# Two layers with 32 experts each: returned rows in the weight stream, one block per expert, selection matmuls for the last four pairs

## The chip, the core and the metric

The kernel runs on one core of a Trainium2 chip. The metric is device time in microseconds. A core has a matmul engine (PE; PEld is its weight load), a vector engine (DVE), a scalar engine (ACT), GpSimd (POOL) and a queue engine (SP) that issues most of the DMAs; a suffix q, as in DVEq, means that engine's own sequencer. Matmuls write to PSUM banks (tiles named `ps` and `psg`).

## The reference, cut to what matters

Two layers work on 512 latent tokens and 256 context tokens of width 1024. Each layer has a mixer (Fourier and convolution in the first, attention in the second) and then a mixture of experts. Layer 0 sends all 768 tokens through the experts, layer 1 only the 512 latent ones. Each token picks a group of 8 experts out of 4 and the best 2 inside it:

```python
h2 = rmsnorm(x, norm_ffn_g[layer]) * (1.0 + sc2) + sh2
...
g_idx = jnp.argmax(g_logit, axis=-1).astype(jnp.int32)
...
top_v, top_i = lax.top_k(e_logit, TOP_K)          # TOP_K = 2, inside the group
w = (g_prob * jax.nn.softmax(top_v, axis=-1)).astype(h.dtype)
...
def expert_block(args):
    xblk, e = args
    return (jax.nn.silu(xblk @ w_gate[e]) * (xblk @ w_up[e])) @ w_down[e]
...
return jnp.zeros((n_tok + 1, d), h.dtype).at[row_tok].add(yb * row_w[:, None])[:n_tok]
...
x = x + g2 * out[: b * s].reshape(x.shape)
```

An expert has 1024 x 512 gate, 1024 x 512 up and 512 x 1024 down weights in f32: two slots of 2 MB (2.10 million bytes) for gate and up, one for down. The 32 experts of a layer are 201 MB. After the second layer comes a final norm.

## The kernel before

The function `moe` (from L869) does the expert part of one layer. It keeps the tokens transposed in `XT` (rows called `xt` in the trace) and puts the normed tokens row by row into a table `h2d` in HBM, whose row 0 is zeros. The router gives every expert 64 slots in a pair's block of 128 rows; `idi` holds, for each pair and slot, the row of `h2d`, 0 for an empty slot. What does not fit into 64 slots goes into the other half of a pair's block a second time (`overflow`) or, beyond that, into spill blocks.

**Weights.** `load_parts` (L960) issues the weights in pinned program order on SP into a ring of eight slots of 2 MB (tiles named `ring`). Per pair of experts the order is gate/up (two slots) of the first, gate/up of the second, down of the first, down of the second. A load waits until the slot it takes is free, and holds all later DMAs of SP's queue. The last three slots of a layer come in halves of 1 MB.

**A pair** (the loop at L1563, 16 a layer). `gather` (L1210, POOL) reads the pair's 128 rows of `h2d` into `xg`, `xpose` transposes them on PE, with copies out by ACT and DVE. `gate_up` (L1345) is 32 matmuls, then silu on ACT (L1353) and two multiplies on DVE (L1357) into `hb`. `turned` (L1360) transposes `hb` twice on PE, with ACT copies (L1366); `down` (L1369) is 16 matmuls; `place` (L1379, DVE L1383) adds the result into `y`; `scatter` (L1429, POOL) writes the rows of `y` to a table `yd` in HBM, skipping empty rows by an index out of range. All matmuls are issued through one helper, so they stand at L56 in the trace. PE's order is pinned as written: gate/up of both experts, with the transposes of the first in the middle of the second's gate/up; then the branch; then DOWN of the first with the transposes of the second in its middle; then `xpose` of the next pair; then DOWN of the second. `gate_up` of a pair's first expert writes a bank `psg`, of the second one of the banks `ps`.

**The branch.** `overflow` (L1513) is a conditional at L1517 on a count that the router found. Every engine comes to it in every pair; it is taken in 7 of 32. Taken, it runs up to two more blocks with the pair's weights (silu of these also at L1353) and, in one pair, spill blocks. Hints to the sequencers (`mark_branch_hint_location`) name PE, DVE and ACT (`HINTED`).

**The end of a layer.** Pairs 0 to 14 are scattered. Pair 15 stays on chip, split into a high and a low part, `yh` and `yl`, and a matrix `sel` that says which token each row belongs to. `fetch_rows` (L1553) is called in pair 15: it reads each token's two returned rows from `yd` into ring slots on SP (1 MB each) and adds the two on DVE (L1560). `token_rstd` (L1460) then goes through the 8 blocks of 128 features: `fetched(m)` transposes the added rows into a bank by matmuls with the identity, four matmuls with `sel` add pair 15 (two in layer 1, which has one segment of tokens), and `add_gated` (L295, DVE) multiplies by the gate and adds to `XT`; ACT squares the result (L1478) for the next norm.

Of the kernel before, what the change touches and what calls it, by code (L numbers as in the profile page):

```python
# [16 lines left out]
P = 128  # L17
# [25 lines left out]


HINTED = [mybir.EngineType.PE, mybir.EngineType.DVE, mybir.EngineType.Activation]
# [17 lines left out]
class Kern:  # L63
# [805 lines left out]
    def moe(self, l, segs, outp, rt, last=False):  # L869
# [9 lines left out]
        with ExitStack() as es:  # L879
# [76 lines left out]
            lq, spare = [], []  # L956
# [3 lines left out]
            def load_parts():  # L960
                for e in range(0, NE, 2):
                    for src in (A["gu"][l, e, 0], A["gu"][l, e, 1], A["gu"][l, e + 1, 0], A["gu"][l, e + 1, 1], A["dn"][l, e], A["dn"][l, e + 1]):
                        a = slot() if len(lq) % 8 != 6 else spare[0].tile([P, 4096], F32, name=self.nm("ring"), tag="ring")
                        for c in ((slice(0, 2048), slice(2048, 4096)) if len(lq) >= 3 * NE - 3 else (slice(0, 4096),)):
                            pin(eng[0].dma_start(out=a[:, c], in_=src[:, c]))
                        lq.append(a)
                        yield

            lg_ = load_parts()

            def load(k):
                for _ in range(k):
                    next(lg_, None)

# [25 lines left out]
            xg = wk.tile([P, D], F32, name="xg", tag="xg")  # L1000
            xs = wk.tile([P, D], F32, name="xs")
            hb = wk.tile([P, D], F32, name="hb")
            k3 = lambda t: t.rearrange("p (k c) -> p k c", k=KD)
            V, S, T, G = (Pinned(tc, e) for e in (nc.vector, nc.scalar, nc.tensor, nc.gpsimd))
            if nv == 2:
                da[1], dsh[0], dsh[1] = (k3(t) for t in (xg, xs, hb))
# [18 lines left out]
            def token_major(t_):  # L1025
                tm = hb if t_ % 3 == 2 else keep([D], tag="y3", bufs=2)
# [181 lines left out]
            V.tensor_copy(idi, idf)  # L1208
# [106 lines left out]
            def weights(e):  # L1315
                b, i = 6 * (e // 2), e % 2
                return ([g.rearrange("p (k c f) -> p k c f", k=4, c=2) for g in lq[b + 2 * i:b + 2 * i + 2]],
                        lq[b + 4 + i].rearrange("p (k d) -> p k d", k=4))

            spills = []  # L1320
# [23 lines left out]

            def gate_up(W, xt, s, wcol, mid=None, bank=None, tag=""):  # L1345
                po = (bank or self.ps)()
                for k in range(KD):
                    if mid and k == KD // 2:
                        mid()
                    for c in range(2):  # L1350
                        T.matmul(po[64 * c:64 * c + 64, :], xt[:, k, s], W[0][k // 4][:, k % 4, c, :], start=k == 0, stop=k == KD - 1)
                sg = keep([256], tag="sg")
                S.activation(sg, po[:, :256], AF.Silu)  # L1353
                h = [hb[:, P * b:P * b + P] for b in ((6, 7) if tag else (0, 1))]
                for b in range(2):
                    cs_ = slice(P * b, P * b + P)
                    V.scalar_tensor_tensor(h[b], sg[:, cs_], wcol, po[:, 256 + P * b:384 + P * b], op0=ALU.mult, op1=ALU.mult)  # L1357
                return h

            def turned(h, tag=""):  # L1360
                ht = []
                for b in range(2):
                    po = self.ps()
                    T.transpose(po[:, :P], h[b], self.ident)
                    ht.append(keep([P], tag=f"ot{b}") if tag == "o" else hb[:, P * (2 + 2 * int(tag) + b):P * (3 + 2 * int(tag) + b)])
                    S.activation(ht[b], po[:, :P], AF.Copy)  # L1366
                return ht

            def down(W, ht, mid=None):  # L1369
                pd = self.ps()  # L1370
                for j, kt in enumerate((0, 2, 1, 3)):
                    if mid and j == 2:
                        mid()
                    for dh in range(2):
                        T.matmul(pd[64 * dh:64 * dh + 64, :], ht[kt % 2][:, 64 * (kt // 2):64 * (kt // 2) + 64],
                                 W[1][:, kt, 512 * dh:512 * dh + 512], start=j == 0, stop=j == 3)
                return pd

            def place(dst, i, pd, add=True):  # L1379
# [25 lines left out]
            def spill_block(W, e, wc):  # L1405
                i = e % 2
                xt = xpose(xs, half(i), "xto", 1)
                pd = down(W, turned(gate_up(W, xt, slice(0, 64), wc, tag="o"), "o"))
# [44 lines left out]
            def fetched(m):  # L1453
                pss_ = [self.ps() for _ in segs]
                for t_ in range(nt):
                    o = P * t_ - segs[vt(t_)][0]
                    T.matmul(pss_[vt(t_)][:, o:o + P], fy[t_][:, P * m:P * m + P], self.ident, start=o == 0, stop=False)
                return pss_

            def token_rstd():  # L1460
# [8 lines left out]
                yh, yl, sel = pend  # L1469
                ahead = fetched(0)  # L1470
                for m in range(KD):
                    pss_, ahead = ahead, fetched(m + 1) if m + 1 < KD else None
                    for z, y in enumerate((yh, yl)):
                        for p, (o, w) in zip(pss_, segs):
                            T.matmul(p[:, :w], y(m), sel(m)[:, o:o + w], start=False, stop=z == 1)
                    for v, (p, (o, w)) in enumerate(zip(pss_, segs)):
                        self.add_gated(m, p, o, w, gate, v)
# [35 lines left out]
            def overflow(pr_, Ws, xt, y, ys, direct):  # L1513
# [3 lines left out]
                with tc.If(spills[pr_ % 8] > 0, label=f"ov{l}_{pr_}"):  # L1517
                    tc.mark_branch_hint_location(f"sp{l}_{pr_}", "LikelyTaken", HINTED)
                    for i in range(2):
                        e = 2 * pr_ + i  # L1520
                        with tc.If(value(1, e, None) > 0):
                            h = gate_up(Ws[i], xt, half(1 - i), wd[:, 1 - i, e:e + 1], tag="o")
                            place(y, 1 - i, down(Ws[i], turned(h, "o")), False)
# [23 lines left out]

# [205 lines left out]
```

## Time and profile before

| what | value |
|---|---|
| runs | 1801.62, 1806.47, 1806.97 us; median 1806.47 |
| the profiled execution | 1808.97 us; its span from first to last instruction 1807.2 us |
| mean granted clock of PE | 0.944 of full speed |
| busy share of the span | PE 85%, PEld 45%, DVE 39%, ACT 23%, POOL 16% |
| moved by DMA | 545.23 MB, mean 302 GB/s |

The busy shares are means over stages with different limits: two mixers and two expert parts. The expert part of layer 0 lies at about 300 to 874 us, that of layer 1 at about 1230 to 1790. What bounds a stage is read from windows and from the waits in that stage. A line of the view of time gives the start, the busy time, the engine, the line, the operation, out<-in, how many, and in brackets the idle time before it and what ended it.

### The profile page before, as it was taken

Reading aid. Unit: us, or ns where it says so; the run is one execution under the profiler, and the core shown is the slowest. Engines: PE = TensorE matmul, PEld = TensorE weight load, DVE = VectorE, ACT = ScalarE, POOL = GpSimd, SP = SyncE. Lnnn points to the kernel's source line nnn. Section 1 sums busy time; section 2 is a strip of 40 time slices with the busy share of each in tenths; the row PEclk is TensorE's granted clock in tenths of the full one; section 3 lists DMA queues with packets and bytes.
Section 4 is the critical chain, followed back from the end, with each engine's and each line's share of the span. In section 5 each row is a group of like instructions: output and inputs, shape, how many; then the busy total and the mean of one; then the engine's idle time right before and its main releaser. Section 6 shows DMA issues by size and latency. Waiting matters only on the chain. (4 is left out here: it accounts for less than half of the span.)

```text
span 1807.2 us, 21981 instructions
## 1 busy us (share of the span) xinstructions
PE 1533.7 (85%) x8285; PEld 816.8 (45%) x8285; DVE 706.2 (39%) x1342; ACT 410.3 (23%) x930; POOL 283.9 (16%) x232
## 2 busy tenths in 40 slices
PE   6997997988788779767898899996897888888776
PEld 4775686332222223223686878784222322223223
DVE  6799867211111101113636876554111211112115
ACT  4211632110100001001445554332110111011012
POOL 1231343001010101000232202022000101101001
PEclk9999998999989989998999999997899998999998
DMA  8997173799999968999221131488989999999991
GB/s 300 316 298 272 51 291 129 315 399 423 409 426 429 427 247 354 429 427 416 97 88 53 54 104 46 141 293 334 396 343 425 426 385 426 426 387 426 428 366 69
DMA packets 90052, 545.23 MB, mean 302 GB/s; under 512 B 10136, under 2 KB 32296, under 8 KB 63792
## 3 DMA queue, kind: packets, MB, share of 16 engines
q1 hardware_dynamic: 80240, 510.55, 70.7%
q0 software_dynamic: 9536, 31.50, 4.5%
q8 instruction: 112, 1.84, 0.4%
q14 instruction: 164, 1.34, 0.2%
HBM read 511.82 MB, written 34.09 MB: 302 GB/s over the span
## 5 line engine op out<-in xcount | busy, mean ns | idle before, releaser
L56 PE MATMUL ps<-ring,mk 128*64 128x512 f32 x1408 | 326.7, 607 | 35.3 <-DMA ring<-gu 27.2
L56 PE MATMUL ps<-ring,hb 128*64 128x512 f32 x1024 | 265.8, 654 | 100.4 <-DVEq L1517 67.0
L56 PE MATMUL psg<-ring,mk 128*64 128x512 f32 x1024 | 235.8, 610 | 24.2 <-DMA ring<-gu 24.2
L1383 DVE TENSOR_TENSOR mk<-ps,mk 64x512 f32<-64x512 f32 x128 | 88.2, 689 | 319.3 <-PE ps L56 299.5
L56 PEld LDWEIGHTS ps<-ring,mk 128*64 128x64 f32 x1408 | 98.1, 139 | 231.0 <-issue 178.8
L56 PEld LDWEIGHTS ps<-ring,hb 128*64 128x64 f32 x1024 | 72.0, 146 | 239.9 <-issue 160.7
L56 PEld LDWEIGHTS psg<-ring,mk 128*64 128x64 f32 x1024 | 77.6, 140 | 175.6 <-issue 173.0
L1357 DVE SCALAR_TENSOR_TENSOR hb<-mk,mk,ps 128x128 f32<-128x128 f32 x80 | 24.2, 345 | 307.5 <-ACT mk L1353 307.5
L510 DVE SCALAR_TENSOR_TENSOR cv<-u,convw,cv 128x798 f32<-128x798 f32 x120 | 139.1, 1215 | 3.5 <-ACT cv L508 3.0
L1357 DVE SCALAR_TENSOR_TENSOR hb<-mk,mk,psg 128x128 f32<-128x128 f32 x64 | 19.4, 345 | 220.5 <-ACT mk L1353 220.5
L1366 ACT ACTIVATE hb<-ps 128x128 f32<-128x128 f32 x128 | 28.9, 275 | 301.5 <-PE ps L56 301.5
L1211 POOL DMA_INDIRECT xg<-h2d,mk x30 | 30.9, 1029 | 391.3 <-PE ps L56 391.3
L1353 ACT ACTIVATE mk<-psg 128x256 f32<-128x256 f32 x32 | 12.3, 383 | 345.2 <-PE psg L56 188.6
L1567 POOL MEMSET mk<- 128x1024 f32 x32 | 30.5, 953 | 307.3 <-DMA yd<-mk,mk 301.2
L111 PE MATMUL ps<-hh,hi 128*128 128x512 f32 (+1 forms) x232 | 71.4, 365 | 7.2 <-ACT hh L285 7.2
L95 POOL TENSOR_TENSOR lo<-wc,hi 128x1024 fp32r<-128x1024 f32 (+3 forms) x25 | 44.0, 1764 | 175.4 <-ACT hi L89 127.4
L113 PE MATMUL ps<-hl,hi 128*128 128x512 f32 (+1 forms) x232 | 68.6, 349 | 0.0
L115 PE MATMUL ps<-hh,lo 128*128 128x512 f32 (+1 forms) x232 | 68.0, 347 | 0.0
L95 POOL TENSOR_TENSOR lo<-wo,hi 128x512 fp32r<-128x512 f32 x32 | 44.6, 1399 | 114.5 <-ACT hi L89 112.9
L1430 POOL DMA_INDIRECT yd<-mk,mk x30 | 30.2, 1007 | 183.5 <-DVE mk L1383 183.5
L111 PE MATMUL ps<-hi,hi 128*128 128x512 f32 (+1 forms) x191 | 57.1, 348 | 2.2 <-DVE ptl L691 2.0
L113 PE MATMUL ps<-lo,hi 128*128 128x512 f32 (+1 forms) x191 | 55.2, 336 | 3.4 <-POOL lo L95 3.4
(372 smaller groups left out, 2328.8 us busy)
## 6 DMA issues: line engine op xcount, KB each, us to landing
ring<-gu SPq DMA_DIRECT2D x125, 2048.0 KB, 24.0
ring<-dn SPq DMA_DIRECT2D x59, 2048.0 KB, 26.8
mw<-modw SPq DMA_DIRECT2D x72, 512.0 KB, 5.7
yd<-mk SPq DMA_DIRECT2D x20, 512.0 KB, 7.6
ring<-yd SPq DMA_DIRECT2D x10, 1024.0 KB, 12.7
mw<-modh SPq DMA_DIRECT2D x16, 512.0 KB, 7.4
ring<-dn SPq DMA_DIRECT2D x8, 1024.0 KB, 23.0
wi<-w_in SPq DMA_DIRECT2D x12, 512.0 KB, 7.8
```

The costliest lines, as they stand in the source:

```text
L56: i = f(*a, **k)
L95: nc.gpsimd.tensor_tensor(lo, src, hi, op=ALU.subtract)
L111: T.matmul(o, lh, rh, start=start, stop=False)
L113: T.matmul(o, lh, rl, start=False, stop=False)
L115: T.matmul(o, ll, rh, start=False, stop=stop)
L510: nc.vector.scalar_tensor_tensor(acc, u[:, j:j + LO], cw[:, j:j + 1], acc, op0=ALU.mult, op1=ALU.add)
L1211: return G.indirect_dma_start(out=xg, out_offset=None, in_=h2d, in_offset=bass.IndirectOffsetOnAxis(ap=idi[:, pr_:pr_ + 1], axis=0), bound ...
L1357: V.scalar_tensor_tensor(h[b], sg[:, cs_], wcol, po[:, 256 + P * b:384 + P * b], op0=ALU.mult, op1=ALU.mult)
L1366: S.activation(ht[b], po[:, :P], AF.Copy)
L1383: V.tensor_tensor(d, p, d, op=ALU.add)
L1430: G.indirect_dma_start(out=yd, out_offset=bass.IndirectOffsetOnAxis(ap=rows, axis=0), in_=y, in_offset=None, bounds_check=2 * n - 1, oob_i ...
L1567: G.memset(y, 0.0)
```

## The change

- `load_parts` issues the weights expert by expert: gate/up (two slots), then down. Behind the weights of experts 28, 29 and, in layer 0, 30 it reads the returned rows of 256 tokens each into a ring slot (`back`). The last two slots of a layer come in halves, not the last three.
- The loop goes through one expert after the other: gate/up, the transposes, DOWN, `place`. The next pair's `xpose` stands between gate/up and the transposes of the second expert. The branch stands behind the first expert. All experts' gate/up write the bank `psg`. The multiplies write into the silu's tile, so `hb` goes.
- Hints name PE alone.
- Pairs 0 to 11 are scattered; 12 to 15 stay on chip. Each is added by `combine` (selection matmuls and `add_gated`) in the next pair's first expert, in three parts (`hooks`); pair 15 in `token_rstd`.
- `merge` adds the two returned rows on POOL, transposes them on PE and adds them to `XT` on DVE (`scalar_tensor_tensor` of 128 x 128), in experts 29, 30 and, in layer 0, 31. `fetched` and `fetch_rows` go.
- `idi` of an empty slot becomes 8192, out of range, so that the gather skips it.
- `y` has three buffers; only its second half is cleared, and the first expert's result is copied in by ACT instead of added.

```diff
             def load_parts():
-                for e in range(0, NE, 2):
-                    for src in (A["gu"][l, e, 0], A["gu"][l, e, 1], A["gu"][l, e + 1, 0], A["gu"][l, e + 1, 1], A["dn"][l, e], A["dn"][l, e + 1]):
-                        a = slot() if len(lq) % 8 != 6 else spare[0].tile([P, 4096], F32, name=self.nm("ring"), tag="ring")
...
+                todo = []
+                for e in range(NE):
+                    todo += [(e, A["gu"][l, e, 0]), (e, A["gu"][l, e, 1]), (e, A["dn"][l, e])]
+                    if 28 <= e < 28 + nt // 2:
+                        todo.append((None, e - 28))
+                for q, (e, src) in enumerate(todo):
+                    a = slot() if q % 8 != 6 else spare[0].tile([P, 4096], F32, name=self.nm("ring"), tag="ring")
+                    if e is None:
+                        v = a.rearrange("p (t q c) -> p t q c", t=2, q=2)
+                        for c in range(2):
+                            o = n * c + 2 * P * src
+                            pin(nc.sync.dma_start(out=v[:, :, c], in_=yd[o:o + 2 * P, :].rearrange("(t p) c -> p t c", p=P)))
+                        back.append(v)
...
-            V.tensor_copy(idi, idf)
+            pad = sm(16)
+            V.tensor_scalar(pad, idf, 0.5, 8192.0, op0=ALU.is_lt, op1=ALU.mult)
+            V.tensor_tensor(idi, pad, idf, op=ALU.add)
...
-                ahead = fetched(0)
                 for m in range(KD):
-                    pss_, ahead = ahead, fetched(m + 1) if m + 1 < KD else None
...
+                    combine([m], *pend)
...
-                    tc.mark_branch_hint_location(f"sp{l}_{pr_}", "LikelyTaken", HINTED)
+                    tc.mark_branch_hint_location(f"sp{l}_{pr_}", "LikelyTaken", [mybir.EngineType.PE])
...
+            def merge(v, t_):
+                G.tensor_tensor(v[:, 0], v[:, 0], v[:, 1], op=ALU.add)
+                for hh in range(2):
+                    po = self.ps()
+                    for q in range(4):
+                        T.transpose(po[:, P * q:P * q + P], v[:, 0, P * (4 * hh + q):P * (4 * hh + q) + P], self.ident)
+                    for q in range(4):
+                        k = 4 * hh + q
+                        x = self.XT[k][:, P * t_:P * t_ + P]
+                        V.scalar_tensor_tensor(x, po[:, P * q:P * q + P], gate[:, k, vt(t_):vt(t_) + 1], x, op0=ALU.mult, op1=ALU.add)
+
...
             for pr_ in range(16):
...
+                direct = pr_ < 12
+                y = keep([D], tag="y3", bufs=3)
+                G.memset(y[64:128], 0.0)
+                for i in range(2):
+                    e = 2 * pr_ + i
+                    load(4 if e == 30 else 3 if e else 1)
...
+                    elif i == 0 and pend:
+                        hooks = [(lambda q=q: combine(q, *pend)) for q in (range(3), range(3, 6), range(6, KD))]
+                    h = gate_up(W, xts[pr_], half(i), wd[:, i, e:e + 1], hooks[0], True)
+                    if hooks[1]:
+                        hooks[1]()
+                    if 29 <= e < 29 + nt // 2:
+                        for t_ in range(2):
+                            merge(back[e - 29][:, t_], 2 * (e - 29) + t_)
+                    if i == 1 and pr_ + 1 < 16:
+                        xts[pr_ + 1] = xpose(xg, slice(0, P), "xt", 2)
+                        if pr_ + 2 < 16:
+                            gather(pr_ + 2)
+                    place(y, i, down(W, h, hooks[2]), i == 1)
+                    if i == 0:
+                        ys = [xs] if direct else [keep([D], F32R, tag="y3", bufs=3) for _ in range(2)]
+                        overflow(pr_, (W, weights(e + 1)), xts[pr_], y, ys, direct)
```

On PE, a pair in the middle of layer 0 stood in this order (the kernel before; the words in brackets are the semaphores waited for; `hb` holds the activations, `mk_5193` is the next pair's transposed rows):

```order
L56 MATMUL ps_5176<-ring_4601,hb 64x512 [waits DVE_49,DMAHW2_49,PE_49,Activation_49]
...
L56 MATMUL ps_5194<-cst,xg 128x128 [waits DMASW6_49,Activation_49]
...
L56 MATMUL ps_5211<-ring_4603,hb 64x512 [waits DMAHW3_49,Activation_49]
...
L56 MATMUL psg_5229<-ring_4620,mk_5193 64x512 [waits DMAHW4_49,Activation_49]
...
L56 MATMUL ps_5253<-ring_5168,mk_5193 64x512 [waits DMAHW6_49]
...
L56 MATMUL ps_5262<-cst,hb 128x128 [waits DVE_49]
...
L1517 COMPARE_AND_BRANCH
```

The same place now: second expert of one pair, then first expert of the next, up to the branch (`mk_5182` and `mk_5250` are activations, `mk_5186` the next pair's transposed rows):

```order
L53 MATMUL psg_5165<-ring_4590,mk_4615 64x512 [waits DMAHW1_49,PE_49]
...
L53 MATMUL ps_5187<-cst,xg 128x128 [waits DVE_49,DMASW6_49,PE_49,Activation_49]
...
L53 MATMUL ps_5202<-cst,mk_5182 128x128 [waits DVE_49]
...
L53 MATMUL ps_5210<-ring_4655,mk_5204 64x512 [waits DMAHW3_49,Activation_49]
...
L53 MATMUL psg_5233<-ring_4657,mk_5186 64x512 [waits DMAHW4_49,PE_49]
...
L53 MATMUL ps_5254<-cst,mk_5250 128x128 [waits DVE_49]
...
L53 MATMUL ps_5262<-ring_5159,mk_5256 64x512 [waits DMAHW6_49,Activation_49]
...
L1515 COMPARE_AND_BRANCH
```

What moved: each expert's transposes and DOWN now follow its own gate/up, ahead of the other expert, and the branch comes after a DOWN instead of after both gate/ups.

On SP, the end of layer 0 before (`gu` and `dn` are weights, `yd_102` the returned rows, `modw` the next layer's modulation weights):

```order
L965 DMA ring_11470<-gu 128x4096
L965 DMA ring_11472<-gu 128x2048 x2
L965 DMA ring_11475<-dn 128x2048 x2
L965 DMA ring_11478<-dn 128x2048 x2
L1558 DMA ring_11580<-yd_102 128x2x1024
L1517 COMPARE_AND_BRANCH
...
L1558 DMA ring_11580<-yd_102 128x2x1024
L1558 DMA ring_11585<-yd_102 128x2x1024 x2
L1558 DMA ring_12246<-yd_102 128x2x1024 x2
L1597 DMA ring_12251<-modw 128x2048 x2
```

And now:

```order
L974 DMA ring_11353<-dn 128x4096
L969 DMA ring_11355<-yd_102 128x2x1024 x2
L974 DMA ring_11358<-gu 128x4096
...
L969 DMA ring_11426<-yd_102 128x2x1024
...
L974 DMA ring_12194<-dn 128x4096
L969 DMA ring_12293<-yd_102 128x2x1024 x2
L974 DMA ring_12296<-gu 128x4096
L974 DMA ring_12298<-gu 128x2048 x2
L974 DMA ring_12301<-dn 128x2048 x2
L1571 DMA ring_13103<-modw 128x2048
```

What moved: the reads of returned rows stand between weights, three slots or more ahead of the last ones, and behind the last weights only `modw` follows.

On PE, the last expert and the start of `token_rstd` in layer 0 before (`mk_12289` is a part of pair 15, `mk_11526` the selection):

```order
L56 MATMUL ps_12274<-ring_11478,hb 64x512 x8
...
L56 MATMUL ps_12298<-cst,ring_11580 128x128 x2
L56 MATMUL ps_12298<-cst,ring_11585 128x128 x2
L56 MATMUL ps_12299<-cst,ring_12246 128x128 x2
...
L56 MATMUL ps_12298<-mk_12289,mk_11526 128x512
L56 MATMUL ps_12299<-mk_12289,mk_11526 128x256
```

And now (`ring_12293` is the last slot of returned rows, `mk_13126` the activations):

```order
L53 MATMUL psg_13109<-ring_12296,mk_12255 64x512 x8
L53 MATMUL psg_13109<-ring_12298,mk_12255 64x512 x8
L53 MATMUL ps_13131<-cst,ring_12293 128x128 x4
...
L53 MATMUL ps_13168<-cst,mk_13126 128x128
...
L53 MATMUL ps_13176<-ring_12301,mk_13170 64x512 x4
...
L53 MATMUL ps_13200<-mk_13191,mk_12447 128x512
L53 MATMUL ps_13201<-mk_13191,mk_12447 128x256
```

What moved: the identity matmuls on returned rows have left the 8 rounds behind the last DOWN, and a part of them stands between gate/up and DOWN of the last expert.

## Rows read from the trace of the kernel before

**Rows 1.** Windows, layer 0: stretch, length, busy PE, PEld, DVE, ACT, POOL, PEclk, DMA share, GB/s

```profile
340.00:650.00 310.00, 260.28 (x1155) 86.52 (x1154) 47.05 (x93) 25.95 (x78) 31.71 (x32) 0.96 1.00 418
690.00:860.00 170.00, 133.92 (x582) 47.63 (x578) 33.49 (x57) 13.31 (x37) 12.24 (x13) 0.92 1.00 421
```

**Rows 2.** Order of time, PE, a pair of layer 0 without overflow

```profile
537.72 7.04 PE L56 MATMUL psg<-ring,mk 128*64 128x512 f32 x32
...
553.58 1.94 PE L56 MATMUL ps<-ring,hb 128*64 128x512 f32 x8 [1.44 <-DVEq L1517]
...
557.68 1.09 PE L56 MATMUL ps<-cst,xg 128*128 128x128 f32 x8
558.70 3.65 PE L56 MATMUL ps<-ring,hb 128*64 128x512 f32 x16
562.27 3.65 PE L56 MATMUL psg<-ring,mk 128*64 128x512 f32 x16
568.08 4.49 PE L56 MATMUL psg<-ring,mk 128*64 128x512 f32 x12 [2.15 <-DMA ring<-gu]
```

**Rows 3.** Windows of ten microseconds at taken overflow branches, both layers

```profile
670.00:680.00 10.00, 8.90 (x40) 2.97 (x42) 0.61 (x2) 0.92 (x3) 0.77 (x1) 1.00 0.08 17
...
1330.00:1340.00 10.00, 7.55 (x34) 2.25 (x32) 0.60 (x2) 2.12 (x5) 0.00 (x0) 1.00 0.26 86
1460.00:1470.00 10.00, 6.27 (x28) 1.89 (x26) 0.61 (x2) 2.12 (x5) 0.00 (x0) 0.99 0.74 280
1590.00:1600.00 10.00, 7.77 (x36) 2.23 (x32) 0.61 (x2) 2.00 (x5) 0.00 (x0) 1.00 0.69 292
1720.00:1730.00 10.00, 7.88 (x36) 2.34 (x32) 0.60 (x2) 1.89 (x5) 0.00 (x0) 1.00 0.73 310
```

**Rows 4.** End of layer 0: last weight half with its landing, then order of time

```profile
L965 SPq DMA_DIRECT2D ring<-dn x1: 328/328/328, 812.4 to 812.4; - x1
...
DMA to landing us min/median/max: 26.0/26.0/26.0
...
859.58 1.50 PE L56 MATMUL ps<-cst,ring 128*128 128x128 f32 x12
860.83 0.94 PE L56 MATMUL ps<-mk,mk 128*128 128x512 f32 x4
871.89 2.19 DVE L295 SCALAR_TENSOR_TENSOR xt<-ps,mod,xt 128x512 f32<-128x512 f32 x4 [0.90 <-PE ps L56]
```

**Rows 5.** End of layer 1: last weight halves with their landing, the last add

```profile
L965 SPq DMA_DIRECT2D ring<-dn x2: 441/472/502, 1733.8 to 1734.4; - x2
...
DMA to landing us min/median/max: 19.9/19.9/19.9
...
1788.97 1.41 DVE L295 SCALAR_TENSOR_TENSOR xt<-ps,mod,xt 128x512 f32<-128x512 f32 x2 [0.61 <-PE ps L56]
```

**Rows 6.** The page's DMA parts: queue (packets, MB, share); issues (count, KB, us)

```profile
q0 software_dynamic: 9536, 31.50, 4.5%
...
ring<-yd SPq DMA_DIRECT2D x10, 1024.0 KB, 12.7
```

**Rows 7.** Order of time, layer 1, pair 2: ahead of and behind the overflow block

```profile
1324.65 0.61 DVE L1357 SCALAR_TENSOR_TENSOR hb<-mk,mk,ps 128x128 f32<-128x128 f32 x2 [6.78 <-ACT mk L1353]
...
1338.29 1.21 ACT L1385 ACTIVATE mk<-ps 64x512 f32<-64x512 f32 x2 [3.48 <-PEq L1524]
...
1339.59 1.94 PE L56 MATMUL ps<-ring,hb 128*64 128x512 f32 x8 [1.40 <-ACTq L1524]
```

**Rows 8.** Order of time inside the overflow block of layer 1, pair 14

```profile
1718.23 5.37 PE L56 MATMUL ps<-ring,mk 128*64 128x512 f32 x24 [0.76 <-issue]
...
1724.52 0.65 PE L56 MATMUL ps<-cst,hb 128*128 128x128 f32 x2 [0.92 <-DVE hb L1357]
...
1725.27 3.65 PE L56 MATMUL ps<-ring,mk 128*64 128x512 f32 x16
```

**Rows 9.** Waits of PE: what for, us in total, times, longest

```profile
PE ps L56 <- DVEq L1517: 67.0, 20, 6.9
```

More of the change, by code (lines that the diff above doesn't have):

```diff
@@ L973, in load, with weights @@
                     next(lg_, None)
+            def weights(e):
+                a = lq[3 * e:3 * e + 3]
+                return ([g.rearrange("p (k c f) -> p k c f", k=4, c=2) for g in a[:2]], a[2].rearrange("p (k d) -> p k d", k=4))
             pG = self.ps(True)
@@ L1315, in weights @@
             def weights(e):
[L1316 to L1320, printed above, removed]
+                a = lq[3 * e:3 * e + 3]
+                return ([g.rearrange("p (k c f) -> p k c f", k=4, c=2) for g in a[:2]], a[2].rearrange("p (k d) -> p k d", k=4))
+            after, spills = [], []
             def xpose(src, rows, tag, bufs):
@@ L1350, in gate_up, with down @@
                     for c in range(2):
[L1351 to L1354, printed above, removed]
+                        i = T.matmul(po[64 * c:64 * c + 64, :], xt[:, k, s], W[0][k // 4][:, k % 4, c, :], start=k == 0, stop=k == KD - 1)
+                        if own and k == 0 and after:
+                            self.after(i, after[-1])
+                sg = keep([2, P], tag="sg")
+                S.activation(sg.rearrange("p b c -> p (b c)"), po[:, :256], AF.Silu)
+                h = [sg[:, b] for b in range(2)]
                 for b in range(2):
-                    cs_ = slice(P * b, P * b + P)
-                    V.scalar_tensor_tensor(h[b], sg[:, cs_], wcol, po[:, 256 + P * b:384 + P * b], op0=ALU.mult, op1=ALU.mult)
+                    V.scalar_tensor_tensor(h[b], h[b], wcol, po[:, 256 + P * b:384 + P * b], op0=ALU.mult, op1=ALU.mult)
                 return h
-            def turned(h, tag=""):
+            def down(W, h, mid=None):
                 ht = []
@@ L1593, in moe @@
+            pend = None
+            for pr_ in range(16):
+                direct = pr_ < 12
[4 more added lines that the diff above has]
+                    load(4 if e == 30 else 3 if e else 1)
+                    if e == NE - 1 and not last:
                         early = []
@@ L1598, in moe @@
                             early += [a[:, D * k:D * k + D] for k in range(4)]
[L1599 to L1606 removed]
+                    W = weights(e)
+                    if i == 0:
+                        tc.mark_branch_hint_location(f"ov{l}_{pr_}", "LikelyTaken", [mybir.EngineType.PE])
@@ L1617, in moe @@
-            pend = (lambda m: yh[:, mc(m)], lambda m: yl[:, mc(m)], lambda m: sel)
+                    continue
+                yh, yl = ys
+                for q in range(2 if pr_ == 15 else 1):
+                    cs_ = slice(512 * q, 512 * q + 512) if pr_ == 15 else slice(0, D)
+                    S.activation(yh[:, cs_], y[:, cs_], AF.Copy)
+                    V.tensor_tensor(yl[:, cs_], y[:, cs_], yh[:, cs_], op=ALU.subtract)
+                sel = keep([n], F32R, tag="S")
+                V.tensor_scalar(sel, self.cst[:, K_IOTA:K_IOTA + n], idf[:, pr_:pr_ + 1], None, op0=ALU.is_equal)
```

114 lines of the change are left out of this document (26 added, 88 removed).

## The prediction

> **What bounds the kernel now.** I read the windows first. In the expert part of layer 0 the DMA share is 1.00 at 418 to 421 GB/s, while PE is busy for 84% and 79% of the two stretches [rows 1]. The expert part is thus bound by the weight stream: one 2 MB slot takes 2.10 MB / 0.42 = 5.0 us, a pair of experts six slots, 30 us, and with its gather and scatter about 31. Next I read PE's order of time for one pair without overflow. Its gate/up starts at 537.72 and the next pair's at 562.27, so PE needs 24.5 us, 1.44 of it a wait at the overflow branch, and then it stands 2.15 us for a weight [rows 2]. So PE has some 6 us of slack a pair, and an edit on PE, DVE or ACT in the middle costs nothing until a pair reaches about 31.
>
> Two kinds of place are not bound by the stream. First the taken overflow branches, seven of 32 pairs (pairs 2, 4, 10 of layer 0; 2, 6, 10, 14 of layer 1): there the DMA share falls [rows 3], so the stream is late for good. Second the two layer ends. In layer 0 the last weight half is issued at 812.4 and lands 26.0 later, at 838.4; the last gated add ends at 871.89 + 2.19 = 874.1, a tail of 35.7 us [rows 4]. In layer 1 the half issued at 1734.4 lands at 1754.3, the last add ends at 1790.4, a tail of 36.1 [rows 5]. What follows the last add is the same in both kernels. So I make the sum as: when does the last weight land in each layer, and how long is the tail behind it.
>
> **The change part by part.** *Returned rows in the stream.* Ten reads of 1 MB [rows 6], six in layer 0 and four in layer 1, ran behind the last weights and now run between them, where the stream is the bound. 6.29 MB / 0.42 = 15.0 us in layer 0 and 4.19 / 0.42 = 10.0 in layer 1, all on the path: **+15.0, +10.0**.
>
> *Order by expert.* Before, the ring of eight slots holds the four gate/up slots of both experts while the overflow block runs, so four loads are outstanding, 20 us of stream, less what had passed when the block began. From the multiplies ahead of the branch, 1324.65, to the DOWN behind the block, 1339.59, are 14.9 us [rows 7]; PE was done with gate/up about 0.5 earlier, so the block takes 15.4. The stretch 1330 to 1340 has a share of 0.26, so 7.4 us idle; the other three stretches of layer 1 give 2.6, 3.1 and 2.7, and in layer 0 the pair with a spill leaves far more than 5 (share 0.08) [rows 3]. After, the first expert is already through DOWN when the block begins. Its three slots are free, the second expert's three are held, so one slot more is outstanding, 5 us. Each idle time shrinks by at most that: 5.0 + 2.6 + 3.1 + 2.7 = 13.4 in layer 1, and 5.0 in layer 0, where I count the spill pair alone. A part can be lost because the second expert is held longer: **-5, -12**; bounds 0 and -18 in all.
>
> *PE with the new order.* An expert's chain is no longer filled by the other one. The overflow block of before shows an unfilled chain: gate/up ends at 1718.23 + 5.37 = 1723.60, DOWN starts at 1725.27, a gap of 1.67 with 0.65 of transposes in it [rows 8]. So an even expert takes 7.04 + 1.67 + 3.65 plus some 0.5 at the branch = 12.9; an odd one has the next pair's transposes (1.09) inside the gap and takes about 12.4 [rows 2, 8]. A pair takes about 25.3, still under 31: **0**. The slack is the cover. If it is gone, every microsecond over 31 is paid 32 times.
>
> *Hints on PE alone.* Before, all three engines get a branch hint, and still PE waits 67.0 us in 20 places for DVE's sequencer at the branch, up to 6.9 [rows 9]. So a skipped branch can cost 6.9 us there even with its hint. After, ACT and DVE have none. But the branch now stands behind the first expert's DOWN, and what waits for ACT and DVE behind it is the second expert's silu, which comes only after its gate/up, 7.04 us on PE [rows 2]. A DVE miss hides there whole; ACT has two copies of about 0.6 in front (1.21 for two [rows 7]), so at worst 1 us of a pair shows, inside PE's slack: **0**. [...]
>
> *Empty rows not gathered.* Top 2 of 32 experts gives 48 tokens of 64 slots on average in layer 0 (768 tokens), 32 in layer 1 (512). The software queue moved 31.50 MB [rows 6]; 32 gathers and 30 scatters of 0.524 MB, the spills (1.05) and two weight loads of 4.19 would be 37.7. The 6.2 missing are the empty rows of the scatters (a quarter and a half of 15 each give 5.9), so a row out of range moves no bytes. The gathers now save the same: 16 x 0.131 MB / 0.42 = 5.0 and 16 x 0.262 / 0.42 = 10.0, of which 14 of 16 pairs lie where the stream binds: **-4.4, -8.7**. Bounds: 0, if a skipped row costs as much as a small one, and the full figure.
>
> *Scatters of pairs 12 to 14 gone.* 3 x 0.39 MB and 3 x 0.26 MB: **-2.8, -1.9**. In their place three pairs per layer are combined by selection matmuls. Eight blocks of four matmuls cost 8 x 0.94 = 7.5 us on PE at most in layer 0 [rows 4], and a merge of two token tiles 16 transposes, 2 x 1.09 = 2.2. Pairs 13 to 15 of layer 0 then take 3 x 25.3 + 3 x 7.5 + 3 x 2.2 = 105 against three pairs of stream and 15 of rows, about 105. PE just keeps up; this cover is thin. DVE gets 8 x 1.1 (four adds take 2.19 [rows 4]) and 16 x 0.3 (two of 128x128 take 0.61 [rows 7]) a pair, under its free time. The ten adds of returned rows move from DVE to POOL, which does little else.
>
> *Tail of layer 0.* Gone are the fetched rows: the reads behind the weights, their adds, and 1.50 of PE in each of eight rounds [rows 4]. Left: gate/up of expert 31 ends about 1 us before the last half lands; merge transposes 2.2, its own 0.65 and a copy, DOWN 3.65, which ends at +5.4; placing 1.4 and splitting 1.3; eight rounds at DVE's 1.1 and one of lead, 9.5. In sum 17.6 against 35.7: **-18.1**.
>
> *Tail of layer 1.* Pair 14 overflows. From the landing of expert 28's down weights PE needs 3.65 + 15.4, then 12.4 + 2.2 for expert 29, 12.9 + 2.2 - 1.0 + 4.7 for expert 30, in all 52.5, while 11 slots (55 us) land; gate/up of 31 (7.04) then ends at +4.5, with 1.67 and 3.65 DOWN at +9.9. Placing and splitting 2.7, eight rounds at 0.7 and one of lead, 6.4: 19 against 36.1: **-17.1**.
>
> *Sum.* Layer 0: +15.0 - 5 - 4.4 - 2.8 - 18.1 = -15.3. Layer 1: +10.0 - 12 - 8.7 - 1.9 - 17.1 = -29.7. Together -45.0, so 1808.97 - 45.0 = 1764.0 for a profiled execution; this one stands 2.5 above the median of the runs, so **1762**.
>
> **Rivals.** *The stream ends later than I say.* If neither the idle time nor the gathers give anything (both have zero as a bound), the stream gets +15.0 - 2.8 and +10.0 - 1.9, and the tails give -35.2: -14.9, so 1792. For it: the idle is an average over ten microseconds, and the second expert's slots are held longer. Against it: the bytes missing from the software queue. *PE is late at the end.* Combine and merge put PE on 105 against 105 in layer 0; if each of the last three pairs meets 2 to 3 us of waits for banks or for DVE's adds, the two tails grow by some 8 each: 1778. *Slower: the expert's own chain becomes the bound.* Place: the transposes ahead of every DOWN, which wait for silu and DVE. Price: PE's pair is 25.3; from the point where waits add more than about 5.7 a pair (a skip over 12 us instead of 6.9, or one of 6 that is not hidden by gate/up) PE sets the pace. Then no slack takes up the overflows: 7 x 15.4 = 108 in place of the roughly 40 lost now, and what I count for idle (17) goes too, so 1762 + 68 + 17 = about 1847. For it: rows 9 and the missing hints. Against it: 7.04 of gate/up stands between. *Nothing moves:* the late PE and the late stream together, about 1805.
>
> **How the numbers follow.** The forecast 0.50; late stream 0.20; late PE 0.15; nothing 0.05; slower 0.10. The measurement tells about 0.3%, 5.4 us, from no change. Faster: 0.50 + 0.20 + 0.15 less a little of the late stream's edge = 0.83; same 0.06; slower 0.11. The range reaches down to 1740: full bounds for idle and gathers (-3), tails 4 shorter each where merge and splitting overlap more (-8), the run 7.4 instead of 2.5 under the profiled time, as the fastest one is (-5), and reads of rows that fall into time idle at an overflow (-5). It reaches up to 1797, just past the late stream.
>
> **What would show it.** Right: no reads of returned rows behind the last weight; the last add 18 to 20 us behind the landing of the last half in both layers; the software queue near 23 MB; DMA share above 0.5 in the overflow stretches of layer 1; the branch no longer among PE's great waits. Wrong: a DMA share clearly under 1 in pairs without overflow (PE sets the pace), PE waiting for DVE's products before the transposes by more than 1 us, or a longer tail with PE busy throughout.

## The result and the profile after

The changed kernel takes 1762.95 us (median; 1760.47 to 1764.76), the kernel before 1804.53 in the runs beside it: a ratio of 0.977 (0.975 to 0.979), 41.6 us less. The forecast was 1762. The profiled execution's span is 1758.7 us against 1807.2, 48.5 less, where the sum said 45.0.

First the page of the kernel after: the busy shares, the software queue, and the reads of returned rows on SP (count, KB, median us to landing).

```profile
span 1758.7 us, 22308 instructions
PE 1535.7 (87%) x8349; PEld 838.2 (48%) x8349; DVE 730.1 (42%) x1444; ACT 451.3 (26%) x990; POOL 302.3 (17%) x236
...
q0 software_dynamic: 8672, 22.98, 3.4%
...
ring<-yd SPq DMA_DIRECT2D x10, 1024.0 KB, 28.3
```

The software queue went from 31.50 MB [rows 6] to 22.98. The ten reads of returned rows are still there, but queue up among weights: 28.3 us from issue to landing against 12.7 [rows 6].

The waits of PE in the kernel after (what for, us in total, times, longest):

```profile
PE psg L53 <- DMA ring<-gu: 35.7, 23, 3.7
PE ps L53 <- DVE mk L1371: 32.0, 35, 0.9
PE psg L53 <- PEq L1515: 17.3, 20, 3.1
...
PE ps L53 <- ACT mk L1380: 13.0, 17, 1.1
...
PE ps L53 <- DMA ring<-gu: 5.3, 2, 4.8
...
PE ps L53 <- DMA ring<-dn: 3.0, 5, 0.8
```

The wait for DVE's sequencer at the branch, 67.0 us before [rows 9], is gone; at the branch (L1515) PE now waits only for its own sequencer, 17.3 us in 20 places. The unfilled chain shows as 32.0 us in 35 waits for the multiplies, never over 0.9, and 13.0 in 17 for ACT's copies of the transposes. And PE waits for weights 35.7 + 5.3 + 3.0 = 44 us, over both layers together. That number turned out to be the important one.

The layer ends of the kernel after: the last down half of layer 0 (issued 813.6) and the last two halves of layer 1 (the landing of the first of these is recorded) with their landings, and the last adds to `XT`.

```profile
L974 SPq DMA_DIRECT2D ring<-dn x1: 2079/2079/2079, 813.6 to 813.6; - x1
...
DMA to landing us min/median/max: 26.4/26.4/26.4
...
L974 SPq DMA_DIRECT2D ring<-dn x2: 328/376/424, 1697.7 to 1698.1; - x2
...
DMA to landing us min/median/max: 21.1/21.1/21.1
...
847.97 8.50 DVE L292 SCALAR_TENSOR_TENSOR xt<-ps,mod,xt 128x512 f32<-128x512 f32 x16
...
1736.56 5.36 DVE L292 SCALAR_TENSOR_TENSOR xt<-ps,mod,xt 128x512 f32<-128x512 f32 x8
```

The start of layer 1's expert part can be read from SP's load of the router weights, `ring<-rw`, first in the kernel before, then after:

```profile
1193.66 0.33 SPq L923 DMA_DIRECT2D ring<-rw  x1
...
1169.72 0.33 SPq L920 DMA_DIRECT2D ring<-rw  x1
```

With these the whole difference falls into five pieces. The last half of layer 1 is set at 1697.7 + 21.1 + 2.4 = 1721.2: the landing recorded is that of the half before it, and 2.4 us is about half of a slot's 5.0, so this entry is an estimate.

| piece | before | after | difference | forecast |
|---|---|---|---|---|
| start to the last weight of layer 0 | 838.4 | 840.0 | +1.6 | +2.8 |
| tail of layer 0, to the last add | 35.7 | 16.5 | -19.2 | -18.1 |
| norm and mixer, to the load of router weights | 319.6 | 313.2 | -6.4 | 0 |
| from there to the last weight of layer 1 | 560.6 | 551.5 | -9.1 | -12.6 |
| tail of layer 1, to the last add | 36.1 | 20.7 | -15.4 | -17.1 |
| sum | | | -48.5 | -45.0 |

So both tails and layer 0 came within 2 us of what was worked out, 5 us were missing in layer 1, and 6 came from a place that I had not counted at all. The experiments look behind these sums, since a sum can be right with wrong terms.

### The profile page after: what moved, and what is told of

Read it like the earlier page. It is cut to its first block, busy times and chain, and to the rows that moved or that the text cites. A ratio compares the mean times of both kernels' runs of the same rounds, so it can differ in the third digit from the quotient of the medians.

```text
span 1758.7 us, 22308 instructions
## 1 busy us (share of the span) xinstructions
PE 1535.7 (87%) x8349; PEld 838.2 (48%) x8349; DVE 730.1 (42%) x1444; ACT 451.3 (26%) x990; POOL 302.3 (17%) x236
## 3 DMA queue, kind: packets, MB, share of 16 engines
q0 software_dynamic: 8672, 22.98, 3.4%
## 5 line engine op out<-in xcount | busy, mean ns | idle before, releaser
L53 PE MATMUL psg<-ring,mk 128*64 128x512 f32 x2048 | 471.1, 610 | 62.3 <-DMA ring<-gu 35.7
L53 PE MATMUL ps<-ring,mk 128*64 128x512 f32 x1408 | 325.4, 606 | 30.7 <-ACT mk L1380 12.7
L53 PEld LDWEIGHTS psg<-ring,mk 128*64 128x64 f32 x2048 | 160.3, 140 | 363.2 <-issue 287.5
L1371 DVE SCALAR_TENSOR_TENSOR mk<-mk,mk,psg 128x128 f32<-128x128 f32 x128 | 38.8, 345 | 538.3 <-ACT mk L1368 538.3
L1395 DVE TENSOR_TENSOR mk<-ps,mk 64x512 f32<-64x512 f32 x74 | 51.0, 689 | 131.5 <-PE ps L53 83.0
L1225 POOL DMA_INDIRECT xg<-h2d,mk x30 | 30.8, 1026 | 409.5 <-PE ps L53 409.5
L292 DVE SCALAR_TENSOR_TENSOR xt<-ps,mod,xt 128x512 f32<-128x512 f32 (+1 forms) x137 | 82.0, 655 | 36.5 <-PE ps L112 26.9
L1562 POOL MEMSET mk<- 64x1024 f32 x32 | 30.4, 950 | 252.2 <-DMA yd<-mk,mk 199.9
L1397 ACT ACTIVATE mk<-ps 64x512 f32<-64x512 f32 x66 | 39.1, 593 | 127.7 <-PE ps L53 60.7
L53 PE MATMUL ps<-cst,mk 128*128 128x128 f32 x144 | 40.6, 321 | 32.0 <-DVE mk L1371 32.0
L53 PE MATMUL ps<-mk,mk 128*128 128x512 f32 (+3 forms) x244 | 51.9, 352 | 17.5 <-DVE mk L53 8.2
L92 POOL TENSOR_TENSOR lo<-wi,hi 128x512 fp32r<-128x512 f32 x24 | 38.4, 1600 | 106.0 <-ACT hi L86 94.2
## 6 DMA issues: line engine op xcount, KB each, us to landing
ring<-yd SPq DMA_DIRECT2D x10, 1024.0 KB, 28.3
```

Source lines behind the costliest of these rows:

```text
L53: i = f(*a, **k)
L92: nc.gpsimd.tensor_tensor(lo, src, hi, op=ALU.subtract)
L292: self.nc.vector.scalar_tensor_tensor(x, ps[:, :w], g[:, m, v:v + 1], x, op0=ALU.mult, op1=ALU.add)
L1225: return G.indirect_dma_start(out=xg, out_offset=None, in_=h2d, in_offset=bass.IndirectOffsetOnAxis(ap=idi[:, pr_:pr_ + 1], axis=0), bound ...
L1371: V.scalar_tensor_tensor(h[b], h[b], wcol, po[:, 256 + P * b:384 + P * b], op0=ALU.mult, op1=ALU.mult)
L1395: V.tensor_tensor(d, p, d, op=ALU.add)
```

## The experiments

All ratios are to the kernel before on the same chip. The changed kernel stands at 0.977; 0.001 is 1.8 us. Each ratio is known to about 0.002, so a difference of two of them to some 5 us.

**Gathers of empty rows, in the changed kernel.** Empty slots read row 0 again.

```diff
-            V.tensor_tensor(idi, pad, idf, op=ALU.add)
+            V.tensor_copy(idi, idf)
```

> The changed kernel, but empty slots read row 0 again, so that every gather moves all 128 rows. My step: the gathers' bytes lie on the bound stream, so the software queue goes from 23.0 back to about 29.5 MB and the time rises by 13.1 us, to about 1776 (ratio to the kernel before near 0.984). Rival, that a skipped row costs as much as a small one: no change, 1763 (0.977). If the transfers only fill idle time at the overflows, 3 to 5 us.

Measured: 1778.2 us, ratio 0.986 (0.983 to 0.988), 16 us above the changed kernel.

**The skip alone, in the kernel before.**

```diff
-            V.tensor_copy(idi, idf)
+            pad = sm(16)
+            V.tensor_scalar(pad, idf, 0.5, 8192.0, op0=ALU.is_lt, op1=ALU.mult)
+            V.tensor_tensor(idi, pad, idf, op=ALU.add)
```

> The kernel before with this one edit: empty slots get an index out of range, so the gathers skip them. My step: 13.1 us less, about 1791 (ratio 0.993), the same as it is worth in the changed kernel. Rival: worth nothing alone (1804), because the time it frees is idle time ahead of an overflow.

Measured: 1795.0 us, ratio 0.994 (0.992 to 0.996), 10 us less than before. The software queue on the two pages, of the changed kernel that gathers all rows and of the kernel before that skips:

```profile
q0 software_dynamic: 8672, 29.67, 4.3%
...
q0 software_dynamic: 9536, 24.81, 3.6%
```

Skipping takes 6.7 MB out of the queue in either kernel and gives 10 and 16 us, around the 13.1 of the sum. A row out of range moved no bytes, and the time went with the bytes. This one edit is about a quarter of the whole gain or more.

**Branch hints on three engines again, in the changed kernel, at both places where hints are set.**

```diff
-tc.mark_branch_hint_location(f"sp{l}_{pr_}", "LikelyTaken", [mybir.EngineType.PE])
+tc.mark_branch_hint_location(f"sp{l}_{pr_}", "LikelyTaken", [mybir.EngineType.PE, mybir.EngineType.DVE, mybir.EngineType.Activation])
...
-tc.mark_branch_hint_location(f"ov{l}_{pr_}", "LikelyTaken", [mybir.EngineType.PE])
+tc.mark_branch_hint_location(f"ov{l}_{pr_}", "LikelyTaken", [mybir.EngineType.PE, mybir.EngineType.DVE, mybir.EngineType.Activation])
```

> The changed kernel with the branch hints on PE, DVE and ACT again. My step: the skips of ACT and DVE lie beside the second expert's gate/up, so no difference, 1763 (within 3 us). Rival: the missing hints cost PE some waits before the transposes, and with them the kernel gets 5 us or more faster.

Measured: 1761.5 us, 0.976 (0.973 to 0.978): no difference. With these hints or without, PE's list of waits has no row for DVE's or ACT's sequencer at the branch: what their skips take is hidden.

**Hints on PE alone, in the kernel before.**

```diff
-HINTED = [mybir.EngineType.PE, mybir.EngineType.DVE, mybir.EngineType.Activation]
+HINTED = [mybir.EngineType.PE]
```

> The kernel before with hints on PE alone. There DOWN waits behind the branch for DVE and ACT. If an unhinted skip stalls for 5 to 7 us each time, PE's wait for DVE's and ACT's sequencers at the branch goes from 67 us to 150 or more, still inside PE's slack of 6 us a pair except at the two layer ends and after overflows: 0 to 15 us slower, 1805 to 1820. If hints on these engines do nothing, the waits stay near 67 and the time at 1804.

Measured: ratio 1.0026 (1.001 to 1.004), 5 us slower. PE's waits at the branch:

```profile
PE ps L56 <- DVEq L1517: 66.4, 19, 7.8
...
PE ps L56 <- ACTq L1517: 17.2, 3, 6.2
```

DVE's share is what it was with hints [rows 9], ACT's rose from 11.0 to 17.2. So the waits at the branch are there with hints and without, and the hints on DVE change nothing that shows. What the waits come from is not shown by any run here. What removes them is another part of the change, since the changed kernel has none, with hints or without. The order by expert, which puts gate/up behind the branch on PE, is the likely one; it was not tried by itself.

**Returned rows neither read nor merged.**

```diff
-                    if 28 <= e < 28 + nt // 2:
-                        todo.append((None, e - 28))
...
-                    if 29 <= e < 29 + nt // 2:
-                        for t_ in range(2):
-                            merge(back[e - 29][:, t_], 2 * (e - 29) + t_)
```

> The changed kernel without the reads of returned rows and without their merge: the rows scattered by pairs 0 to 11 are left out of the result. My step: 25.0 us of stream go, and the tail of layer 0 loses 2 us of merge: 1763 - 27 = about 1736. Rival: the rows travel in time that the stream has idle anyway, so only 5 to 10 us go, about 1755.

Measured: 1749.0 us, 0.969 (0.967 to 0.971): 14 us less, between the two. The merges on PE, POOL and DVE are in these 14 as well. In layer 0 the last weight now lands at 828.7, 11.3 earlier, but the last add ends only 8.2 earlier. PE's order of time at the last expert says why:

```profile
820.21 3.65 PE L53 MATMUL ps<-ring,mk 128*64 128x512 f32 x16
824.42 7.09 PE L53 MATMUL psg<-ring,mk 128*64 128x512 f32 x32 [0.55 <-PEq L1513]
832.41 0.65 PE L53 MATMUL ps<-cst,mk 128*128 128x128 f32 x2 [0.91 <-DVE mk L1369]
833.11 3.65 PE L53 MATMUL ps<-ring,mk 128*64 128x512 f32 x16
```

There is no wait for a weight: with the rows out of the stream PE sets the end. The rows cost 14 us, not 25, because the rest lies beside PE's own work.

**Returned rows behind the last weights, the rest kept.**

```diff
-                    if 28 <= e < 28 + nt // 2:
-                        todo.append((None, e - 28))
+                todo += [(None, j) for j in range(nt // 2)]
...
+                    if e == NE - 1:
+                        load(9)
...
-                    if 29 <= e < 29 + nt // 2:
-                        for t_ in range(2):
-                            merge(back[e - 29][:, t_], 2 * (e - 29) + t_)
...
                     place(y, i, down(W, h, hooks[2]), i == 1)
+                    if e == NE - 1:
+                        for t_ in range(nt):
+                            merge(back[t_ // 2][:, t_ % 2], t_)
```

> The changed kernel with the reads of returned rows behind the last weights, as in the kernel before, and all merges behind the last DOWN; the rest is kept. It splits the gain between the place of the rows and the rest. Without the rows the kernel took 14 us less, and reading them behind the weights costs their landing and merge at the end: of 15.0 and 10.0 us of reads some 9 and 9 lie behind the last DOWN's end, and the 16 transposes and adds of the last two tiles add some 6 in layer 0 and 5 in layer 1: 1749 + 25 to 30 = 1774 to 1779, so the place is worth 11 to 16 us of the 42. Rival: the reads hide under the lag of PE in the last pairs, and the place is worth under 5, 1763 to 1768.

Measured: 1773.1 us, 0.982 (0.980 to 0.984), about 9 us above the changed kernel, a little under the 11 to 16 expected. Behind the last DOWN PE waits for POOL's adds of the rows, tile after tile:

```profile
836.80 1.09 PE L53 MATMUL ps<-cst,ring 128*128 128x128 f32 x8 [0.43 <-POOL ring L1545]
839.12 1.09 PE L53 MATMUL ps<-cst,ring 128*128 128x128 f32 x8 [1.23 <-POOL ring L1545]
841.77 1.09 PE L53 MATMUL ps<-cst,ring 128*128 128x128 f32 x8 [1.55 <-POOL ring L1545]
844.08 1.97 PE L53 MATMUL ps<-cst,ring 128*128 128x128 f32 x8 [1.22 <-POOL ring L1545]
```

So the place of the rows in the stream, with that of their merges on PE, is worth some 9 us of the 42.

**Rows of layer 1 one expert later.**

```diff
+                r0 = 28 if nt > 4 else 29
...
-                    if 28 <= e < 28 + nt // 2:
-                        todo.append((None, e - 28))
+                    if r0 <= e < r0 + nt // 2:
+                        todo.append((None, e - r0))
```

(and the merge likewise, from expert 30 in layer 1)

> The changed kernel with layer 1's two reads of returned rows one expert later (behind experts 29 and 30, merged in 30 and 31). In the trace of the changed kernel the overflow block of pair 14 waits 4.8 us for the second expert's weights, which stand behind 5 us of returned rows. If that wait is what the idle time there comes from, it goes, and the last weight lands 3 to 5 us earlier; the merge in expert 31 gives back about 1: 1759 to 1761. Rival: the block only waits elsewhere, no change within 2 us.

Measured: 1764.7 us, 0.979 (0.977 to 0.981): no gain. The first fence line is PE at the overflow block of pair 14 in the changed kernel, the second in this one:

```profile
1672.88 9.75 PE L53 MATMUL ps<-ring,mk 128*64 128x512 f32 x32 [4.76 <-DMA ring<-gu]
...
1674.01 8.78 PE L53 MATMUL ps<-ring,mk 128*64 128x512 f32 x32 [3.71 <-PEq L1520]
```

The named wait is gone, a wait of 3.7 us, put down to PE's own sequencer, is left, and the block's 32 matmuls still take longer than 7.1. That its weights have only begun to land there in either case would explain it, but this was not tried by itself.

**Selection matmuls of pairs 12 to 14 left out.**

```diff
-                    elif i == 0 and pend:
+                    elif False:
```

> The changed kernel without the selection matmuls of pairs 12 to 14 (their results are left out; pair 15 stays). If PE is thin in the last three pairs, as the late-PE rival has it, the tails get shorter and 5 to 16 us go, 1747 to 1758. My step: they lie beside the stream in layer 0, and in layer 1, behind the overflow of pair 14, up to 5 us of them delay the last expert: 0 to 5 us less, 1758 to 1763.

Measured: 1756.6 us, 0.974 (0.972 to 0.977): about 5 us less, at the edge of what can be told. The cover is thin, as the forecast said, but it holds for most of the added work, some 22 us on PE in layer 0 alone by the forecast.

**The overflow branch never taken, before and after.** The blocks and the spills are left out.

```diff
-                with tc.If(spills[pr_ % 8] > 0, label=f"ov{l}_{pr_}"):
+                with tc.If(spills[pr_ % 8] > 1000, label=f"ov{l}_{pr_}"):
```

> The kernel before with the overflow branch never taken (tokens beyond an expert's 64 slots are left out). The idle time of the stream at the seven taken branches goes, 22 us in layer 0 and 18 in layer 1, and the tail of layer 1 keeps its length: 40 us less, about 1764. Rival: the slots are late for another reason, and less than 25 us go.

> The changed kernel with the overflow branch never taken. If the order by expert had regained 17 us of idle time as I counted, the changed kernel would lose only 23 at the branches here, and, since PE is no longer late in pair 14, some 4 of tail: 1763 - 27 = 1736. By its trace only 9 of the 40 were regained (idle 5.9 less in layer 0, 3.2 less in layer 1): then 31 + 4 go, about 1728.

Measured: 1765.1 us, ratio 0.980 (0.977 to 0.982), and 1729.2, ratio 0.959 (0.957 to 0.962). The branches cost the kernel before 37 us and the changed one 32. So the whole change gave back about 5 us of the 40 at the branches, give or take 7, not 17. The changed kernel without overflow shows one more thing, how much PE then waits for weights:

```profile
PE psg L53 <- DMA ring<-gu: 107.2, 68, 5.4
...
PE ps L53 <- DMA ring<-dn: 6.5, 11, 0.8
```

It is 114 us in place of 44: the overflow blocks use up most of the slack that PE would have.

**More work on PE: all gate/up matmuls of every second expert twice, then half of them twice.**

```diff
-                for k in range(KD):
+                for k in (list(range(KD)) * 2 if own and s.start == 64 else range(KD)):
...
-                for k in range(KD):
+                for k, z in ([(q, q == 3) for q in range(4)] if own and s.start == 64 else []) + [(q, q == KD - 1) for q in range(KD)]:
```

> The changed kernel with the 32 gate/up matmuls of every second expert of a pair issued twice (the second pass overwrites the first with the same values): PE gets 7.0 us more a pair, 32.4 instead of 25.3, against 30 to 31 of stream. My rival of the expert's chain as the bound, put on by hand: beyond 31 PE sets the pace and no slack takes up the overflows. 32 x 1.5 = 48 and some 60 to 70 of overflow, about +115, 1878. If PE had more slack than I read (stream still the bound), +15 to +40.

> The changed kernel with 8 of the 32 gate/up matmuls of every second expert issued twice: about 1.8 us more on PE a pair, 27 instead of 25.3, against 30 to 31 of stream. My step, 5.7 us of slack in every pair, gives no change (1763 to 1766). The reading after the double dose (183 us more for 225 us of added work) is that PE has only some 40 us of slack over both layers, since the overflow blocks and the last pairs use up the rest: 32 x 1.8 = 58 us of added work then cost 20 to 40, 1783 to 1803.

Measured: 1946.0 us, ratio 1.078 (1.074 to 1.083), and 1833.8, ratio 1.016 (1.014 to 1.017). The second text has the dose wrong: four of eight steps are half of gate/up, not a quarter. The trace of that kernel has 48 matmuls in 10.52 us instead of 32 in 7.04:

```profile
566.52 10.52 PE L53 MATMUL psg<-ring,mk 128*64 128x512 f32 x48 [0.61 <-PEq L1515]
```

So the dose was 3.5 us a pair, 111 us in all, and cost 71; the double one (13.95 us for 64 matmuls) was 221 us and cost 183. They absorb 40 and 38 us, near the 44 that PE waits for weights in the changed kernel. And those waits are what was used up: in the half-dose kernel PE no longer waits for gate/up weights at all, and of its waits for weights this row alone is left:

```profile
PE ps L53 <- DMA ring<-dn: 0.8, 1, 0.8
```

The reading in the second text, some 40 us of slack over both layers, gives 71 for the true dose, which is what was measured. In the half-dose kernel a pair without overflow takes 28.5 us, well under the stream's 30 to 31, and the kernel is nevertheless slower than before.

## Why the prediction was right, and where its steps were not

*The tails* (-18.1 and -17.1 forecast, -19.2 and -15.4 measured) carry the change, and the steps hold: no rows behind the weights, the eight rounds bound by DVE's adds (8.50 us for sixteen against 9.5 with their lead), the pair with overflow late in layer 1. Of the signs named, the tails missed the stated 18 to 20 us by little on either side (16.5 and 20.7).

*Empty rows* (-13.1): right, 10 and 16 us by experiment.

*Hints* (0): right; the cover named, gate/up behind the branch, fits what the runs show. PE's pair was right too: where there is neither an overflow nor a wait for weights, silu to the silu two experts later is 25.0 us in layer 0 and 25.8 in layer 1, forecast 25.3.

*Returned rows* (+25.0): mis-sized. 14 us by leaving them out, since in the last three pairs PE is as late as the stream; the step said "all on the path", and the path was shared.

*Scatters* (-4.7): not tried by itself.

*Idle time at the branches* (-17): the step that failed. Windows of the kernel after at the branches, a pair of layer 0 with a spill, then pairs 2, 10 and 14 of layer 1 (stretch, length, busy PE, PEld, DVE, ACT, POOL, PEclk, DMA share, GB/s):

```profile
660.00:670.00 10.00, 8.63 (x40) 2.87 (x42) 0.61 (x2) 1.23 (x4) 0.94 (x1) 1.00 0.08 17
1300.00:1310.00 10.00, 8.17 (x38) 2.95 (x38) 1.98 (x4) 0.94 (x3) 0.00 (x0) 1.00 0.53 193
1550.00:1560.00 10.00, 8.11 (x38) 2.66 (x36) 1.98 (x4) 0.94 (x3) 0.00 (x0) 1.00 0.68 260
1680.00:1690.00 10.00, 8.18 (x39) 2.55 (x36) 2.14 (x5) 0.94 (x3) 2.43 (x2) 1.00 0.32 108
```

Set against [rows 3], the pair at 1330 went from 7.4 us idle to 4.7, the one at 1590 stayed at 3.1 to 3.2, the one at 1720 rose from 2.7 to 6.8, a share under the 0.5 that was named as a sign; only at pair 6 (2.6) did it vanish. The forecast said that the first expert's slots are free during the block. They are not: the block is given the weights of both experts, and in pair 14 SP's next loads stand right behind the end of its DOWN:

```profile
1684.23 3.65 PE L53 MATMUL ps<-ring,mk 128*64 128x512 f32 x16
...
1688.02 0.82 SPq L974 DMA_DIRECT2D ring<-gu  x2
```

And the branch now comes so early that a block may wait for its second expert's weights, 4.76 us in pair 14. Over the 500 us or so up to the last weight of a layer, the idle time of the DMA engines fell from 21.6 to 17.1 us in layer 0, where 5 less were forecast, and from 20.0 to 16.5 in layer 1, where 12 less were. So layer 1 is where the step failed. The trace thus says some 8 us for both layers, the kernels without overflow 5; how the rest divides among the pairs stays open.

*Slack of PE.* "PE has some 6 us of slack a pair, and an edit on PE, DVE or ACT in the middle costs nothing until a pair reaches about 31" was wrong, and the rival's turning point with it. Overflow blocks and the last pairs use the slack up: PE is held up by weights for 44 us in 32 pairs, 1.4 a pair. The rival's price of 85 us for being bound by PE was too small as well: a pair of 28.5 us cost 71 and one of 31.9 cost 183, so one of 31 would cost some 150, an estimate on the line between the two. The mechanism came about as described, only much sooner: 3.5 us a pair were enough. The forecast was safe because the change adds little to PE in the middle, not because there was room.

*What came from outside.* The 6.4 us between the layers have two parts, and the forecast had neither. The first, 2.5 us, lies in the norm behind the last add: its next step on DVE comes 7.9 us behind that add before (874.1 to 881.99) and 5.4 after (856.47 to 861.90). ACT's first step in it, before and after:

```profile
879.75 0.60 ACT L546 ACTIVATE y<-psg 128x512 f32<-128x512 f32 x1 [1.78 <-PE ps L184]
...
859.65 0.60 ACT L543 ACTIVATE y<-psg 128x512 f32<-128x512 f32 x1 [0.47 <-PE psg L53]
```

Before, the trace puts the wait down to PE's next matmuls. All four traces with the old order have this wait, and of the ten with the new order one (the double dose). So "what follows the last add is the same" held for the instructions, not for what they wait for; why the wait comes and goes stays open.

The other 3.9 us begin at one instruction of the mixer, whose code is the same. DVE's `tensor_scalar` on `pr` takes 2.25 us before while POOL adds beside it, and 0.61 after, where POOL's add is the long one:

```profile
1019.42 2.25 DVE L674 TENSOR_SCALAR pr<-pr,st 128x768 f32<-128x768 f32 x1
1019.45 1.81 POOL L95 TENSOR_TENSOR lo<-kr,hi 128x768 fp32r<-128x768 f32 x1 [0.62 <-ACT hi L89]
...
999.23 0.61 DVE L671 TENSOR_SCALAR pr<-pr,st 128x768 f32<-128x768 f32 x1
999.28 2.25 POOL L92 TENSOR_TENSOR lo<-kr,hi 128x768 fp32r<-128x768 f32 x1 [0.64 <-ACT hi L86]
```

Behind it PE waits 2.04 us for DVE, and its granted clock falls, to 0.88 of full speed on average where it is 1.00 after. The ten microseconds around it, before and after:

```profile
1015.00:1025.00 10.00, 6.17 (x33) 5.03 (x33) 9.05 (x18) 5.81 (x16) 5.58 (x3) 0.88 0.00 1
...
995.00:1005.00 10.00, 7.82 (x51) 6.59 (x50) 8.22 (x21) 7.48 (x22) 5.89 (x3) 1.00 0.01 2
```

PE is busy for 6.2 of these 10 us. In windows of one microsecond its granted clock is 0.85 at 1022, 0.50 at 1023, 1024 and 1025, and 0.95 at 1026; in the kernel after it is 1.00 in each from 995 to 1007. The long instruction costs 1.7 us; the lower clock and what follows make 3.9 of it by the load of the router weights. It is in seven of the fourteen traces, two with the old order and five with the new (PE's longest wait for `ptl` there is 2.0 us in each of these, and 0.4 in the kernel after), so it is luck of the two profiled executions and not a gain of the change. They differ by 48.5 us where the medians of the runs differ by 41.6; this can be 3.9 of those 6.9, and the rest was not traced.

The two errors, rows too dear by 11 and idle time regained too large by 9 to 12, cancelled, and that was luck. The total was right to 1 us; two of its terms were not. A little more luck lies in the start: the saving is 41.6, not 45.0, but the kernel before took 1804.53 us beside the changed one and 1806.47 in the runs that the forecast started from.

Taken one at a time the edits tried are worth 16 us (empty rows), 9 (place of the rows) and 5 (branches) of the 42. They need not add up, and the rest, scatters and the shorter rounds of the tails among it, was not split further.

## What to carry to other kernels

Take the slack of an engine from all its waits for the bounding resource over the whole stage, not from one undisturbed period: rare long blocks use up what every period saves. Adding work to that engine in two doses shows how much is left. Where two engines come to the end of a stage together, as PE and the stream did here in the last three pairs, a cost taken from one of them is paid or gained only in part. An index out of range was a cheap way to take bytes from the gathers (6.7 MB, at an issue time of 1026 ns against 1029), and reads that nothing waits for yet belonged here in front of the last weights, not behind them.

## What the runs showed of the hardware

A skipped branch held PE up at DVE's sequencer for as long without hints on DVE as with them, 66.4 us against 67.0; at ACT's it was 17.2 against 11.0. An indirect gather with rows out of range kept its issue time on POOL (1026 ns on average against 1029 before) while the bytes fell by 6.7 MB: the saving is all in the transfer. And where a DVE instruction on 128 x 768 and a POOL add on 128 x 768 began within 0.05 us of each other, one of the two took longer, DVE (2.25 us against 0.61) in the kernel before or POOL (2.25 against 1.81) in the kernel after, in the same code.
